# Rotary on VectorE, shared banks read once, and later VectorE halves in the attention mixers of a two-layer decoder

## The chip, the cores and the metric

The kernel runs on one core of a Trainium2 chip. The metric is the device time of one execution in microseconds (us). Unless a number is called a median, it comes from one profiled execution of the kernel; the medians come from runs without a profile.

## What is computed

The input is 256 tokens of width 1024 in fp32. Two layers follow each other; each is a SwiGLU half-step, an attention mixer and a second SwiGLU half-step, every one with an RMSNorm ahead of it and a residual sum behind it. A final RMSNorm ends it. Cut to what matters here:

```python
def partial_rotary(t, pos):                 # first 16 of the 64 columns of every head
    x1, x2 = tf[..., :half], tf[..., half:ROT_DIM]
    out = jnp.concatenate([x1 * cos - x2 * sin, x1 * sin + x2 * cos, tf[..., ROT_DIM:]], axis=-1)

for layer in range(2):
    h = h + 0.5 * swiglu(rmsnorm(h, ffn1_norm[layer]), ...)      # 1024 -> 2816 -> 1024
    hn = rmsnorm(h, mix_norm[layer])
    h = h + (mixer_a(hn, ...) if layer == 0 else mixer_b(hn, ..., shared_k, shared_v))
    h = h + 0.5 * swiglu(rmsnorm(h, ffn2_norm[layer]), ...)
    if layer == 0:
        shared = shared_kv(h, kv_norm, kv_w, pos)
```

With 256 tokens both mixers come down to attention of 16 heads of 64 columns over 256 keys with an additive mask. In mixer A queries, keys and values come from the same normalised stream; in mixer B keys and values come from the stream after layer 0 (with its own norm), queries from the stream of layer 1. Rotary is applied to queries and keys.

## The kernel before, in words

**Split products.** Every fp32 product is made of three fast TensorE matmuls. An operand is split in a rounded part (`hi`, or `wh` for a weight) and a rest (`lo`, `wl`), and `product` (lines 176 to 183) adds hi·hi, hi·lo and lo·hi. ScalarE makes the rounded part by a copy, VectorE the rest by a subtraction that reads source and rounded part: `parts_of` (line 86) for activations, `pieces_of` (line 143) for weights. So a VectorE subtraction always waits for the ScalarE copy of the same tile.

**Stages.** The program runs first half-step, mixer A, half-step, half-step, mixer B, half-step. The half-steps multiply weights as 128x512 matmuls (lines 190 and 193). Only the mixers concern the change; in the profile they lie at about 194 to 342 us and 700 to 838 us.

**A mixer** (line 532) works in four groups `g` of four heads, and in two token tiles `t` of 128 tokens. For a group, `projections` (line 588) yields one product step after another: queries and keys side by side in one 512-wide accumulator per token tile in mixer A (`qk_a`), and the values of both token tiles in the two halves of a third accumulator (`v_a`). In mixer B keys and values share the 512-wide accumulators (`kv_b`) and the queries of both token tiles share one (`q_b`); its last group takes keys, queries and values by themselves (`k_b`, `q_b`, `v_b`). An accumulator is one PSUM bank; there are five of them and three further banks (`trt`) for transposes and scores, each reused in turn.

When a projection is complete, `evacuate` (line 571) reads it: values are split by `parts_of` into `vs`; queries and keys are copied by ScalarE into `turns` (tile `rt`), and when both are there `rotate` (line 456) turns the first 16 columns of every head by four small GpSimd operations (lines 463 to 466). `turn_in` (line 552) transposes `rt` on TensorE (`qt`) and splits the result into `qkh` and `qkl`.

**Attention** (line 468) works on pairs `p` of heads. `scores` multiplies queries and keys (`s`), adds the mask and takes the row minimum on VectorE (line 491), takes the exponential and its sum on ScalarE (line 494), inverts the sums on VectorE (line 496) and scales the rows on GpSimd (line 499). `turn` transposes the result (`pt`) and splits it (`pT`). `values` multiplies it with the values: both heads of a pair have one half each of the accumulator `po`; each half is read by ScalarE and VectorE (lines 522, 523) before the matmuls of the other head, and the sum `oT` is split and appended to `blocks`. `out_t` (line 421) multiplies `blocks` with the output weights.

**What sets the order.** Every engine takes its own instructions strictly in order; semaphores join the engines. The order of the calls is written by `Agenda` (line 252): a clock `now` advances by the cost that each product step yields (0.68 us for a 512-wide step), and a call entered with `after(wait, ...)` is issued when the clock has passed its time. `turn_in` is due 3.6 after its rotary, and when the second token tile is in, `scores`, `turn` and `values` of two pairs are entered with waits from 3.0 to 20.7. `out_t` yields `None` while a block is missing, and the next call is then taken at once. `Pieces` (line 274) splits the weights `LEAD` = 4 pieces ahead of their product step and issues their loads on SP's queue two units ahead of that.

## Time and profile before

| | before |
|---|---|
| median of 3 runs | 1037.94 us (1036.07 to 1038.06) |
| profiled execution, its time | 1037.39 us |
| profiled execution, its span | 1035.3 us |
| instructions in the span | 15836 |
| mean granted TensorE clock | 0.987 of full speed |
| HBM traffic | 174 MB read, 1 MB written, 169 GB/s over the span |

The profile gives for each engine (PE is TensorE's matmul side, PEld its weight loads, DVE VectorE, ACT ScalarE, POOL GpSimd) the busy time and the number of instructions. Its other views, each introduced where it is used, are: a list of waits (which engine's which instruction waited for whom, total, times and longest, in us); a timeline (start and duration in us, engine, source line, operation, tiles written and read, and in brackets the idle time ahead of it and what ended it); groups of instructions of one line and shape (busy time, mean ns of one); and sums over stretches of time (busy time and number of instructions of each engine, the granted clock, the share of the DMA engines, GB/s). Line numbers in profile rows are those of the kernel of that profile. Durations of matmuls include their drain, so two successive starts, not the duration, give the pace.

### The profile page before, as it was taken

How to read it: one execution, taken by the hardware profiler on the slowest of the kernel's cores; microseconds unless marked ns; L12 is line 12 of the kernel's file. 1: busy time of each engine (PE TensorE's matmuls, PEld its weight loads, DVE VectorE, ACT ScalarE, POOL GpSimd, SP SyncE). 2: the span in 40 equal slices, each digit the busy share in tenths (PEclk: the TensorE clock that was granted, in tenths of full speed). 3: DMA queues.
4: the chain of work that ended last, by engine and by line, in shares of the span. 5: the costliest groups of instructions: out<-in, count | busy, mean ns of one | idle time of the engine just before them, and what ended most of it. 6: DMA issues, size and time to landing. Idle time of an engine off the chain costs nothing. (4 is left out here: it accounts for less than half of the span.)

```text
span 1035.3 us, 15836 instructions
## 1 busy us (share of the span) xinstructions
PE 996.0 (96%) x5947; PEld 875.6 (85%) x5947; DVE 714.4 (69%) x1188; ACT 592.7 (57%) x1092; POOL 221.9 (21%) x275
## 2 busy tenths in 40 slices
PE   8999999989879999999999999999898999999997
PEld 5888888878779888888888888888777898888886
DVE  7978866655556787775768877665655677878642
ACT  6765664466456566664546566544665666566531
POOL 3111111252333221110112111111534422111000
PEclk9999999999889999999999999999999999999999
DMA  9775565643223466556655654665433344664521
GB/s 308 257 245 181 183 207 192 200 143 116 82 82 123 163 201 199 170 183 205 195 190 163 193 197 160 213 203 191 146 123 100 104 134 151 204 203 167 205 77 41
DMA packets 158396, 176.05 MB, mean 170 GB/s; under 512 B 3568, under 2 KB 152304, under 8 KB 158320
## 3 DMA queue, kind: packets, MB, share of 16 engines
q1 hardware_dynamic: 157888, 174.50, 50.8%
q8 instruction: 46, 0.75, 0.3%
q10 hardware_dynamic: 432, 0.55, 0.2%
q14 instruction: 30, 0.25, 0.1%
HBM read 173.99 MB, written 1.05 MB: 169 GB/s over the span
## 5 line engine op out<-in xcount | busy, mean ns | idle before, releaser
L190 PE MATMUL f_g<-x_n,wh_f_g 128*128 128x512 f32 x688 | 180.1, 394 | 0.0
L190 PE MATMUL f_u<-x_n,wh_f_u 128*128 128x512 f32 x688 | 177.7, 391 | 2.3 <-DVE j_f_g L321 2.3
L339 POOL TENSOR_TENSOR j_f_u<-j_f_u,r_n 128x256 f32<-128x256 f32 x88 | 77.2, 879 | 381.8 <-DVE j_f_u L321 357.7
L190 PEld LDWEIGHTS f_u<-x_n,wh_f_u 128*128 128x128 f32 x688 | 128.8, 188 | 30.2 <-issue 2.1
L190 PEld LDWEIGHTS f_g<-x_n,wh_f_g 128*128 128x128 f32 x688 | 124.0, 189 | 22.6
L190 PE MATMUL dn_f<-act_f,wh_f 128*128 128x512 f32 x528 | 126.5, 391 | 0.0
L151 DVE TENSOR_TENSOR wl_f_u<-raw_f_u,wh_f_u 128x1024 fp32r<-128x1024 f32 x86 | 119.2, 1387 | 2.8 <-ACT wh_f_u L150 2.7
L151 DVE TENSOR_TENSOR wl_f_g<-raw_f_g,wh_f_g 128x1024 fp32r<-128x1024 f32 x86 | 103.4, 1232 | 19.8 <-PE f_g L193 13.9
L190 PEld LDWEIGHTS dn_f<-act_f,wh_f 128*128 128x128 f32 x528 | 96.8, 188 | 18.6
L151 DVE TENSOR_TENSOR wl_f<-raw_f,wh_f 128x1024 fp32r<-128x1024 f32 x72 | 81.8, 1153 | 35.9 <-ACT wh_f L150 26.7
L193 PE MATMUL f_g<-x_n,wl_f_g 128*128 128x256 f32 x688 | 103.4, 282 | 0.0
L193 PE MATMUL f_u<-x_n,wl_f_u 128*128 128x256 f32 x688 | 103.4, 283 | 0.0
L193 PEld LDWEIGHTS f_g<-x_n,wl_f_g 128*128 128x128 f32 x688 | 96.9, 190 | 6.5
L150 ACT ACTIVATE wh_f<-raw_f 128x1024 fp32r<-128x1024 f32 x72 | 67.3, 978 | 49.5 <-PE dn_f L190 27.2
L150 ACT ACTIVATE wh_f_u<-raw_f_u 128x1024 fp32r<-128x1024 f32 x86 | 86.6, 1046 | 15.0 <-PE f_g L190 10.9
L150 ACT ACTIVATE wh_f_g<-raw_f_g 128x1024 fp32r<-128x1024 f32 x86 | 89.5, 1048 | 9.9 <-issue 6.0
L193 PEld LDWEIGHTS f_u<-x_n,wl_f_u 128*128 128x128 f32 x688 | 91.7, 192 | 0.5 <-DVE wl_f_u L151 0.4
L227 POOL TENSOR_TENSOR ss_n<-ss_n,sq_n 128x256 f32<-128x256 f32 x42 | 41.2, 982 | 210.0 <-ACT sq_n L226 209.0
L88 ACT ACTIVATE act_f<-j_f_g 128x256 fp32r<-128x256 f32 x88 | 36.5, 417 | 71.3 <-DVE j_f_g L340 71.1
L337 ACT ACTIVATE j_f_g<-j_f_g 128x256 f32<-128x256 f32 x88 | 36.8, 418 | 63.1 <-DVE j_f_g L336 62.7
L193 PEld LDWEIGHTS dn_f<-act_f,wl_f 128*128 128x128 f32 x528 | 68.1, 191 | 2.8
L193 PE MATMUL dn_f<-act_f,wl_f 128*128 128x256 f32 x528 | 69.0, 283 | 0.0
(211 smaller groups left out, 1869.3 us busy)
## 6 DMA issues: line engine op xcount, KB each, us to landing
raw_f_g<-in_ffn_w_gate_dram SPq DMA_DIRECT2D x43, 1024.0 KB, 5.2
raw_f_u<-in_ffn_w_up_dram SPq DMA_DIRECT2D x43, 1024.0 KB, 5.2
raw_f<-in_ffn_w_down_dram SPq DMA_DIRECT2D x24, 1024.0 KB, 4.8
raw_f_d<-in_ffn_w_down_dram SPq DMA_DIRECT2D x11, 1024.0 KB, 4.9
raw_f<-in_ffn_w_down_dram SPq DMA_DIRECT2D x12, 768.0 KB, 4.2
raw_qka<-in_a_w_qkv_dram SPq DMA_DIRECT2D x16, 512.0 KB, 4.3
raw_kvb<-in_kv_w_dram SPq DMA_DIRECT2D x12, 512.0 KB, 4.2
raw_va<-in_a_w_qkv_dram SPq DMA_DIRECT2D x4, 1024.0 KB, 5.0
```

Of the source, the lines that this page charges most:

```text
L88: nc.scalar.activation(hi, src, AF.Copy, scale=scale)
L150: nc.scalar.activation(wh, r, AF.Copy)
L151: nc.vector.tensor_sub(wl, r, wh.bitcast(F32))
L190: nc.tensor.matmul(ac, wh, flat(x), start=first and i == 0, stop=False)
L193: nc.tensor.matmul(ac[:, :S], wl, x[:, 0, :], start=False, stop=last and i == len(ws) - 1)
L227: nc.gpsimd.tensor_tensor(self.ss, self.ss, sq, op=ALU.add)
L337: nc.scalar.activation(g, g, AF.Silu)
L339: nc.gpsimd.tensor_tensor(u, u, norm.row, op=ALU.mult)
```

## The change

Five edits, all of them in or for the mixers:

- `rotate` issues its four operations on VectorE, not on GpSimd, and it is entered in the agenda 0.7 after the copy; `turn_in` is due 3.2 after the copy, not 3.6.
- `evacuate` of accumulators that two token tiles share is called when both are complete, so that no matmul goes to a bank between two reads of it; queries and keys that lie side by side are copied in one 512-wide ScalarE operation; in `kv_b` the values are read ahead of the keys.
- `values` issues the matmuls of both heads, then both reads; the VectorE sum, the split of `oT` and its entry in `blocks` become calls of the agenda 0.7, 1.4 and 2.2 later.
- `scores` hands the exponentials (`soften`) and the scaling (`scale`) to the agenda, one head at a time, with a reciprocal for each head.
- The VectorE half of a split is entered 0.7 later (`later=agenda.soon`) in the mixers, and in `Pieces` the subtraction of one piece is issued after the copy of the next one.

`run_next` also sets the clock forward to the time of the call that it takes. The loads on SP's queue stand in the same order in both programs, and away from the mixers every engine's instructions stand in the same order.

```diff
-    def parts_of(hi, lo, src, scale=1.0):
+    def parts_of(hi, lo, src, scale=1.0, later=None):
+        def rest():
+            ...
         nc.scalar.activation(hi, src, AF.Copy, scale=scale)
+        (later or (lambda call: call()))(rest)
...
+        def soon(self, call):
+            self.after(0.7, call)
         def run_next(self):
-            _, call, args = self.calls.pop(0)
+            at, call, args = self.calls.pop(0)
+            self.now = max(self.now, at)
...
-                self.parts.append(pieces_of(f"{name}_{j}", self.raws[u][:, j * k:j * k + k], k, n))
+                nc.scalar.activation(wh, raw, AF.Copy)
+                self.parts.append([(wh[:, r, :], wl[:, r, :]) for r in range(k)])
+                self.rest.append(lambda wl=wl, raw=raw, wh=wh: nc.vector.tensor_sub(wl, raw, wh.bitcast(F32)))
+                while len(self.rest) > (m < end - 1):
+                    self.rest.pop(0)()
...
-        nc.gpsimd.tensor_tensor(ta, v[:, :, :ROT], cs, op=ALU.mult)
-        nc.gpsimd.tensor_tensor(tb[:, :, :HALF], v[:, :, HALF:ROT], sn[:, :, :HALF], op=ALU.mult)
-        nc.gpsimd.tensor_tensor(tb[:, :, HALF:], v[:, :, :HALF], sn[:, :, HALF:], op=ALU.mult)
-        nc.gpsimd.tensor_tensor(v[:, :, :ROT], ta, tb, op=ALU.add)
+        nc.vector.tensor_mul(ta, v[:, :, :ROT], cs)
+        nc.vector.tensor_mul(tb[:, :, :HALF], v[:, :, HALF:ROT], sn[:, :, :HALF])
+        nc.vector.tensor_mul(tb[:, :, HALF:], v[:, :, :HALF], sn[:, :, HALF:])
+        nc.vector.tensor_add(v[:, :, :ROT], ta, tb)
...
+                agenda.after(0.7 + 0.7 * i, soften, sm, nm[:, i], ls[:, i])
+        def soften(sm, nm, ls):
+            ...
+            agenda.after(1.3, scale, sm, ls)
+        def scale(sm, ls):
+            nc.vector.reciprocal(ls, ls)
+            for t, seg in enumerate(segs):
+                nc.gpsimd.tensor_scalar(sm[:, seg], sm[:, seg], ls[:, t:t + 1], None, op0=ALU.mult)
...
+            for own, ac in zip(owns, acs):
                 nc.scalar.activation(s[own], ac[DH:], AF.Copy)
+            agenda.soon(lambda: close(p, s, acs))
+        def close(p, s, acs):
+            for own, ac in zip(owns, acs):
                 nc.vector.tensor_add(s[own], ac[:DH], s[own])
             x = atile([P, 2, S], F32R, name=f"oT_{name}{p}")
-            parts_of(x[:, 0], x[:, 1], s)
+            agenda.soon(lambda: parts_of(x[:, 0], x[:, 1], s, later=agenda.soon))
+            agenda.after(1.5, arrived, x)
...
                 if not missing:
-                    rotate(turns[g, t], t, f"{name}{g}_{t}")
-                    agenda.after(3.6, turn_in, g, t)
+                    agenda.soon(lambda: rotate(turns[g, t], t, f"{name}{g}_{t}"))
+                    agenda.after(3.2, turn_in, g, t)
...
-                            if k0 + 2 * k == KD:
+                            if k0 + 2 * k == KD and wide == 512:
                                 evacuate(g, t, norm.col[t], acs[t], parts, missing[t])
                         i += 2
+                    if wide < 512:
+                        for t in range(NT):
+                            evacuate(g, t, norm.col[t], acs[t], parts, missing[t])
```

The waits of the entries in `turn_in` stay, but for the second `scores` of the first three groups, which is due at 8.0, not 8.5.

More of the change, by code (lines that the diff above doesn't have):

```diff
@@ L84, in flat @@
         return ap.rearrange("p c n -> p (c n)")
-    def parts_of(hi, lo, src, scale=1.0):
+    def parts_of(hi, lo, src, scale=1.0, later=None):
+        def rest():
+            if isinstance(scale, float):
+                nc.vector.tensor_sub(lo, src, hi.bitcast(F32))
+            else:
+                nc.vector.scalar_tensor_tensor(lo, src, scale, hi.bitcast(F32), op0=ALU.mult, op1=ALU.subtract)
         nc.scalar.activation(hi, src, AF.Copy, scale=scale)
-        if isinstance(scale, float):
-            nc.vector.tensor_sub(lo, src, hi.bitcast(F32))
-        else:
-            nc.vector.scalar_tensor_tensor(lo, src, scale, hi.bitcast(F32), op0=ALU.mult, op1=ALU.subtract)
+        (later or (lambda call: call()))(rest)
     def etile(name, dt=F32):
@@ L278, in __init__ @@
         def __init__(self, specs):
-            self.specs, self.raws, self.parts = specs, [], []
+            self.specs, self.raws, self.parts, self.rest = specs, [], [], []
         def load(self, u):
@@ L289, in split @@
         def split(self, i):
-            while len(self.parts) <= min(i, 2 * len(self.specs) - 1):
-                u, j = divmod(len(self.parts), 2)
+            end = 2 * len(self.specs)
+            while len(self.parts) <= min(i, end - 1):
+                m = len(self.parts)
+                u, j = divmod(m, 2)
                 self.load(u + 2)
@@ L294, in split @@
                 k //= 2
-                self.parts.append(pieces_of(f"{name}_{j}", self.raws[u][:, j * k:j * k + k], k, n))
+                raw = self.raws[u][:, j * k:j * k + k]
+                wh, wl = [wp.tile([P, k, n], F32R, tag=tag, name=f"{tag}_{name}_{j}") for tag in ("wh", "wl")]
+                nc.scalar.activation(wh, raw, AF.Copy)
[3 more added lines that the diff above has]
+                    self.rest.pop(0)()
         def __getitem__(self, i):
@@ L462, in rotate, with attention @@
         tb = sp.tile([P, n, ROT], F32, tag="rotb", name=f"rb_{name}", bufs=2)
-        nc.gpsimd.tensor_tensor(ta, v[:, :, :ROT], cs, op=ALU.mult)
-        nc.gpsimd.tensor_tensor(tb[:, :, :HALF], v[:, :, HALF:ROT], sn[:, :, :HALF], op=ALU.mult)
-        nc.gpsimd.tensor_tensor(tb[:, :, HALF:], v[:, :, :HALF], sn[:, :, HALF:], op=ALU.mult)
-        nc.gpsimd.tensor_tensor(v[:, :, :ROT], ta, tb, op=ALU.add)
-    def attention(operands, mask, name, blocks):
+        nc.vector.tensor_mul(ta, v[:, :, :ROT], cs)
+        nc.vector.tensor_mul(tb[:, :, :HALF], v[:, :, HALF:ROT], sn[:, :, :HALF])
+        nc.vector.tensor_mul(tb[:, :, HALF:], v[:, :, :HALF], sn[:, :, HALF:])
+        nc.vector.tensor_add(v[:, :, :ROT], ta, tb)
+    def attention(agenda, operands, mask, name, blocks):
         segs = [slice(t * P, t * P + (t + 1) * P) for t in range(NT)]
@@ L492, in scores @@
                                                    op0=ALU.add, op1=ALU.min, accum_out=nm[:, i, t:t + 1])
-                for t, seg in enumerate(segs):
-                    nc.scalar.activation(sm[:, seg], sm[:, seg], AF.Exp, bias=nm[:, i, t:t + 1], scale=-1.0,
-                                         accum_out=ls[:, i, t:t + 1])
-            nc.vector.reciprocal(flat(ls), flat(ls))
-            for i in range(2):
-                for t, seg in enumerate(segs):
-                    nc.gpsimd.tensor_scalar(sms[p, i][:, seg], sms[p, i][:, seg], ls[:, i, t:t + 1], None, op0=ALU.mult)
+                agenda.after(0.7 + 0.7 * i, soften, sm, nm[:, i], ls[:, i])
+        def soften(sm, nm, ls):
+            for t, seg in enumerate(segs):
+                nc.scalar.activation(sm[:, seg], sm[:, seg], AF.Exp, bias=nm[:, t:t + 1], scale=-1.0,
+                                     accum_out=ls[:, t:t + 1])
+            agenda.after(1.3, scale, sm, ls)
+        def scale(sm, ls):
+            nc.vector.reciprocal(ls, ls)
+            for t, seg in enumerate(segs):
+                nc.gpsimd.tensor_scalar(sm[:, seg], sm[:, seg], ls[:, t:t + 1], None, op0=ALU.mult)
         def turn(p, i):
@@ L504, in turn @@
                 nc.tensor.transpose(tr[:, n * P:(n + 1) * P], sms[p, i][:, n * P:(n + 1) * P], ident)
-            pT = pp.tile([P, 2, 3 * P], F32R, tag="pT", name=f"pT_{name}{p}_{i}")
-            parts_of(pT[:, 0], pT[:, 1], tr)
-            pTs[p, i] = pT
+            pT = pTs[p, i] = pp.tile([P, 2, 3 * P], F32R, tag="pT", name=f"pT_{name}{p}_{i}")
+            parts_of(pT[:, 0], pT[:, 1], tr, later=agenda.soon)
         def values(p):
@@ L513, in values @@
             vs = operands(g)[1]
-            for i, own in enumerate(owns):
+            acs = [po[:, i * S:(i + 1) * S] for i in range(2)]
+            for i, ac in enumerate(acs):
                 pT = pTs[p, i]
                 v0, v1 = [flat(v[:, 2 * b + i]) for v in vs]
-                ac = po[:, i * S:(i + 1) * S]
                 for n in range(2):
@@ L521, in values, with arrived @@
                     nc.tensor.matmul(ac[:, P:], v1, pT[:, n, S:], start=False, stop=n == 1)
+            for own, ac in zip(owns, acs):
                 nc.scalar.activation(s[own], ac[DH:], AF.Copy)
+            agenda.soon(lambda: close(p, s, acs))
+        def close(p, s, acs):
+            for own, ac in zip(owns, acs):
                 nc.vector.tensor_add(s[own], ac[:DH], s[own])
             x = atile([P, 2, S], F32R, name=f"oT_{name}{p}")
-            parts_of(x[:, 0], x[:, 1], s)
+            agenda.soon(lambda: parts_of(x[:, 0], x[:, 1], s, later=agenda.soon))
+            agenda.after(1.5, arrived, x)
+        def arrived(x):
             blocks.append(x)
@@ L549, in mixer @@
         agenda = Agenda()
-        scores, turn, values = attention(lambda g: (qks[g], vss[g]), mask, name, blocks)
+        scores, turn, values = attention(agenda, lambda g: (qks[g], vss[g]), mask, name, blocks)
         def turn_in(g, t):
@@ L559, in turn_in @@
                 nc.tensor.transpose(tr[:, k * P:(k + 1) * P], s[:, k * P:(k + 1) * P], ident)
-            parts_of(*[x[:, :, t, :] for x in qks[g]], tr.rearrange("p (k n) -> p k n", n=P))
+            parts_of(*[x[:, :, t, :] for x in qks[g]], tr.rearrange("p (k n) -> p k n", n=P), later=agenda.soon)
             if t == NT - 1:
                 p = 2 * g
-                for wait, call, args in ((3.0, scores, (p,)), (8.5, scores, (p + 1,)), (11.0, turn, (p, 0)),
+                for wait, call, args in ((3.0, scores, (p,)), (8.0, scores, (p + 1,)), (11.0, turn, (p, 0)),
                                          (12.3, turn, (p, 1)), (15.0, values, (p,)), (17.0, turn, (p + 1, 0)),
@@ L571, in evacuate @@
         def evacuate(g, t, r, ac, parts, missing):
-            for m, (kind, _, _) in enumerate(parts):
-                src = ac[:, m * n:(m + 1) * n]
-                if kind == "v":
-                    v = atile([P, HG, 2, DH], F32R, name=f"vs_{name}{g}_{t}")
-                    vss.setdefault(g, []).append(v)
-                    parts_of(v[:, :, 0], v[:, :, 1], src.rearrange("p (j d) -> p j d", d=DH), r)
-                    continue
-                if (g, t) not in turns:
-                    turns[g, t] = atile([P, 2 * HG, DH], name=f"rt_{name}{g}_{t}")
-                slots = slice(0, HG) if kind == "q" else slice(HG, 2 * HG)
-                nc.scalar.activation(flat(turns[g, t][:, slots]), src, AF.Copy, scale=r)
-                missing.discard(kind)
+            if (g, t) not in turns:
+                turns[g, t] = atile([P, 2 * HG, DH], name=f"rt_{name}{g}_{t}")
+            kinds = [kind for kind, _, _ in parts]
+            if kinds[-1] == "v":
+                v = atile([P, HG, 2, DH], F32R, name=f"vs_{name}{g}_{t}")
+                vss.setdefault(g, []).append(v)
+                src = ac[:, (len(kinds) - 1) * n:]
+                parts_of(v[:, :, 0], v[:, :, 1], src.rearrange("p (j d) -> p j d", d=DH), r, later=agenda.soon)
+                kinds.pop()
+            if kinds:
+                slots = turns[g, t][:, 0 if kinds[0] == "q" else HG:HG if kinds[-1] == "q" else 2 * HG]
+                nc.scalar.activation(flat(slots), ac[:, :len(kinds) * n], AF.Copy, scale=r)
+                missing.difference_update(kinds)
                 if not missing:
-                    rotate(turns[g, t], t, f"{name}{g}_{t}")
-                    agenda.after(3.6, turn_in, g, t)
+                    agenda.soon(lambda: rotate(turns[g, t], t, f"{name}{g}_{t}"))
+                    agenda.after(3.2, turn_in, g, t)
         def projections():
@@ L606, in projections @@
                                 yield 0.68 if wide == 512 else 0.36
-                            if norm.col is None and (t == NT - 1 or k0 + 2 * k == KD):
+                            if norm.col is None and t == NT - 1:
                                 norm.finish()
-                            if k0 + 2 * k == KD:
+                            if k0 + 2 * k == KD and wide == 512:
                                 evacuate(g, t, norm.col[t], acs[t], parts, missing[t])
                         i += 2
+                    if wide < 512:
+                        for t in range(NT):
+                            evacuate(g, t, norm.col[t], acs[t], parts, missing[t])
         agenda.run(projections())
```

## The prediction

> **What bounds the kernel now.** I read the page's busy times first, then TensorE's waits, then the stretches around the longest of them.

> ```profile
> span 1035.3 us, 15836 instructions
> PE 996.0 (96%) x5947; PEld 875.6 (85%) x5947; DVE 714.4 (69%) x1188; ACT 592.7 (57%) x1092; POOL 221.9 (21%) x275
> ```

> TensorE is busy for 96% of the span and sets the end; its idle time is 39 us. The list of its waits says where (engine, instruction, releaser, then total, times and longest):

> ```profile
> PE qt_a L559 <- POOL rt_a L466: 10.2, 4, 3.4
> PE qt_b L559 <- POOL rt_b L466: 7.7, 3, 3.0
> PE q_b L179 <- ACT rt_b L582: 2.8, 4, 1.6
> PE po_b L519 <- DVE o_b L523: 2.2, 2, 1.9
> PE v_a L179 <- DVE vs_a L92: 2.1, 3, 0.8
> PE po_a L519 <- DVE o_a L523: 1.9, 4, 1.1
> ```

> All six rows lie in the two mixers. The first two, 17.9 us, are the transpose of queries and keys waiting for the rotary on GpSimd. The other four, 9.0 us, are matmuls that wait to write one half of a bank while ScalarE or VectorE still reads the other half. Together 26.9 us.

> One of the long ones in the timeline, GpSimd first, then TensorE:

> ```profile
> 225.47 3.94 POOL L499 TENSOR_SCALAR sm_a<-sm_a,ls_a 128x128 f32<-128x128 f32 x4 [1.11 <-DVE ls_a L496]
> 229.38 0.45 POOL L463 TENSOR_TENSOR ra_a<-rt_a,rot 128x128 f32<-128x128 f32 x1
> 229.79 1.30 POOL L464 TENSOR_TENSOR rb_a<-rt_a,rot 128x64 f32<-128x64 f32 x1
> 231.05 0.32 POOL L465 TENSOR_TENSOR rb_a<-rt_a,rot 128x64 f32<-128x64 f32 x1
> 231.44 0.45 POOL L466 TENSOR_TENSOR rt_a<-ra_a,rb_a 128x128 f32<-128x128 f32 x1
> ...
> 231.95 1.11 PE L559 MATMUL qt_a<-ident,rt_a 128*128 128x128 f32 x4 [3.21 <-POOL rt_a L466]
> ```

> The rotary stands on GpSimd's queue behind 3.94 us of softmax scaling, itself takes 2.5 us, and TensorE stands still for 3.21 us.

> A stall costs more than its length. Sums over stretches (length, PE, PEld, DVE, ACT and POOL busy, granted clock):

> ```profile
> 230.82:231.95 1.13, 0.00 (x0) 0.00 (x1) 0.09 (x1) 0.00 (x0) 1.05 (x4) 0.50 0.00 0
> 231.95:237.65 5.70, 5.70 (x27) 5.70 (x28) 1.11 (x2) 0.98 (x2) 1.37 (x4) 0.50 0.51 184
> 262.78:268.37 5.59, 5.59 (x26) 5.59 (x27) 1.11 (x2) 0.98 (x2) 1.37 (x4) 0.50 0.50 188
> 293.67:299.09 5.42, 5.42 (x26) 5.42 (x27) 1.11 (x2) 0.98 (x2) 1.37 (x4) 0.50 0.59 193
> 814.50:817.91 3.41, 3.41 (x18) 3.41 (x17) 2.17 (x11) 2.43 (x9) 1.37 (x2) 0.50 0.02 5
> ...
> 755.00:782.00 27.00, 23.52 (x170) 20.29 (x169) 16.49 (x38) 17.64 (x41) 11.57 (x16) 1.00 0.33 116
> ```

> Within each of the three long stalls of mixer A the granted clock falls to half, and it stays there for 5.4 to 5.7 us of matmul work behind the stall. In mixer B a stall of 3.0 us costs no clock (last row, which holds one), but the `po_b` wait of 1.9 us is followed by 3.41 us at half. Work at half clock takes twice its time, so half of 5.70 + 5.59 + 5.42 + 3.41 = 20.1 us is lost: 10.1 us.

> **The change part by part.**

> *Rotary off GpSimd.* This removes the cause of the 17.9 us. VectorE has no such small rotary row, so I bound it by its nearest rows:

> ```profile
> L496 DVE RECIPROCAL ls_a<-ls_a 128x4 f32<-128x4 f32 x8 | 1.4, 177 | 4.9 <-ACT sm_a L494 4.9
> L243 DVE TENSOR_SCALAR diag_n<-ident,c_n 128x128 f32<-128x128 f32 x8 | 1.9, 284 | 3.1 <-POOL c_n L236 3.1
> L336 DVE TENSOR_TENSOR j_f_g<-j_f_g,r_n 128x256 f32<-128x256 f32 x88 | 39.5, 452 | 1.2
> ```

> Four elements take 177 ns, 128 take 284 ns and 256 take up to 452 ns; so four operations take between 0.7 us (4 x 177) and 1.8 us (4 x 452). I take 1.0 us (2 x 284 and 2 x about 220 for the 64-element ones, between the first two rows). A group has two rotaries, so VectorE gets 2.0 us more per group. The row of one group period of mixer A, from one qt stall to near the next:

> ```profile
> 238.70:269.50 30.80, 26.55 (x160) 22.73 (x158) 17.14 (x39) 17.27 (x41) 11.82 (x16) 0.89 0.29 103
> 370.00:690.00 320.00, 319.56 (x1839) 282.00 (x1839) 238.14 (x365) 182.90 (x310) 46.68 (x51) 1.00 0.58 191
> ```

> Without its long stall (3.4 us), its `v_a` wait (0.7) and its half clock (half of 5.59, 2.8) this period is 23.9 us; VectorE then has 17.1 + 2.0 = 19.1 us in it, 80%, and ScalarE's 17.3 us are 72%. In the half-steps (second row) VectorE is busy for 238 of 320 us, 74%, and TensorE never waits. So VectorE is covered, but with a margin of less than 5 us per group, and it takes its work in order.

> Is the rotary in time? The rows for the pace (successive starts) of matmuls, of six transposes and of half a `po`; for the way from the mask to the last exponential of a pair (its first and last row, 14 between); and for copies and a subtraction:

> ```profile
> 239.50 0.40 PE L179 MATMUL qk_a<-wh_qka,x_n 128*128 128x512 f32 x1
> 239.73 0.39 PE L181 MATMUL qk_a<-wl_qka,x_n 128*128 128x512 f32 x1
> ...
> 242.10 0.28 PE L181 MATMUL v_a<-wl_va,x_n 128*128 128x256 f32 x1
> 242.22 0.28 PE L183 MATMUL v_a<-wh_va,x_n 128*128 128x256 f32 x1
> ...
> 742.35 0.82 PE L504 MATMUL pt_b<-ident,sm_b 128*128 128x128 f32 x6
> 742.92 0.47 PE L179 MATMUL kv_b<-wh_kvb,x_kx 128*128 128x512 f32 x1
> ...
> 237.85 0.48 PE L519 MATMUL po_a<-pT_a,vs_a 128*128 128x256 f32 x2
> 238.17 0.34 PE L521 MATMUL po_a<-pT_a,vs_a 128*128 128x128 f32 x2
> 238.34 0.62 PE L504 MATMUL pt_a<-ident,sm_a 128*128 128x128 f32 x4
> ...
> 217.16 0.28 DVE L491 CUSTOM_DVE_ANT_0 sm_a<-s_a,masks 128x128 f32<-128x128 f32 x1
> ...
> 219.16 0.19 ACT L494 ACTIVATION_READ_ACCUMULATOR sm_a<-sm_a,nm_a 128x1 f32 x1
> ...
> L582 ACT ACTIVATE rt_b<-q_b,c_n 128x256 f32<-128x256 f32 x8 | 3.8, 470 | 3.8 <-POOL c_n L236 2.4 <-PE q_b L183 1.4
> L88 ACT ACTIVATE qkh_a<-qt_a 128x512 fp32r<-128x512 f32 x8 | 4.8, 598 | 14.5 <-PE qt_a L559 14.5
> L151 DVE TENSOR_TENSOR wl_qka<-raw_qka,wh_qka 128x1024 fp32r<-128x1024 f32 x16 | 19.6, 1231 | 8.7 <-ACT wh_qka L150 8.3
> ```

> In mixer A count from the end of the first token tile's `qk`. TensorE has 12 matmuls of the other tile, six transposes and six value matmuls before `qt`: 12 x 0.23 + 0.57 + 6 x 0.12 = 4.0 us. The scores of a pair end nine matmuls (2.1 us) before that point; mask and exponentials take 219.35 - 217.16 = 2.2 us, and a weight subtraction may hold them up by half its length, 0.6 us: ScalarE is free at 0.7 us, the 512-wide copy takes 0.6 and the rotary 1.0, ready at 2.3 us. Slack 1.7 us: one weight subtraction of 1.23 us in front of it would still be hidden, two would not. In mixer B the order on VectorE puts one weight subtraction between the last two operations of the second token tile's rotary: ready at about 0.1 + 0.9 (two copies) + 1.8 (seven operations) + 1.2 = 4.0 us, TensorE there after 9 x 0.23 + 0.98 (`po`, twice 238.34 - 237.85) + 6 x 0.23 + 0.3 = 4.7 us. Slack 0.7 us. In its last group VectorE has the mask rows of a pair in between as well, and I get 0.3 to 0.5 us too late.

> *Banks read when complete.* Takes the 9.0 us away: no matmul goes to those banks between two reads. In its place the reads come later, so banks come free later. The copies in front of `qt` are two short ones (0.9 us, above). I see no bank reused within 2 us of its read among the five accumulators; among the three transpose banks one pair in mixer B (scores behind `pt_b`) is within 0.3 us.

> *VectorE's half a step later.* Splits reach TensorE later by one piece of four (a piece feeds 12 matmuls, 12 x 0.23 = 2.7 us, so three pieces, 8 us, remain as lead). Source tiles come free a piece later too, so SP issues the next load later; the queue's order stays, a load lands in 4.3 us (row below) and is issued two units, some 11 us, ahead.

> ```profile
> raw_qka<-in_a_w_qkv_dram SPq DMA_DIRECT2D x16, 512.0 KB, 4.3
> ```

> What the edit buys is that VectorE's head-of-line waits for ScalarE (8.7 us in the `wl_qka` row) shrink, which is what makes room for the rotary. I cost it at nothing; its cover is that lead, and if it were gone the price would be up to one 1.23 us subtraction per piece.

> *The softmax by heads.* 16 more reciprocals at 177 ns, 0.35 us per group, inside the 4.8 us left of VectorE's group. The first head's scaling starts about 1 us earlier.

> *The half clock.* It goes with the stalls: 10.1 us.

> *What stays.* I expect some four places with 0.3 to 0.5 us (three in mixer B, one at the end of mixer A), 1.5 us, and as much again for places where the in-order queue is later than my count: 3 us, with no extra half clock. From below it is 0; from above, with half a microsecond at each of the 16 turn-ins, 8 us, and with a half-clock stretch of 3.41 us (1.7 us lost) behind two of them 11.4 us.

> Sum: the profiled execution took 1037.39 us; 1037.39 - 26.9 - 10.1 + 3.0 = 1003.4 us. Its time lies 0.55 us under the median of 1037.94 us, which changes nothing here. I predict **1003.5 us**.

> [...]

> **The rivals.**

> *VectorE becomes late.* The stall moves from GpSimd's queue to VectorE's: at 80% and in order, the rotary stands behind a subtraction that waits for ScalarE. For it: the slack of 0.7 us in mixer B and the 8.7 us that VectorE waits at `wl_qka`. Against it: the half-steps at 74% without any wait. Price: 0.5 us at 16 turn-ins and the clock as above, 11.4 in place of 3 us: **1012 us**.

> *The bank waits stay.* If what makes TensorE wait is not the read between two halves but the reader's lateness, the 9.0 us only move to the next user of the bank, and the half clock behind `po_b` (1.7 us) with them: 1003.5 + 10.7 = **1014 us**. Against it: five accumulators, and after the change the next user of a bank comes a projection later. This is also the case in which that edit does not do what it says.

> *Slower.* In the timeline above one 64-element rotary operation took 1.30 us where its twin took 0.32 us, while VectorE ran a subtraction: the two disturb each other. Should the strided rotary cost VectorE as much, 4 x 1.3 = 5.2 us each, a group gets 10.4 us more and VectorE needs 17.1 + 10.4 = 27.5 us; if it still waits for others in 4.8 of the 13.7 us that it is idle now, that makes 32.3 us against a period of 30.8 us before. Eight groups then lose 1.5 us each: 1037.4 + 12 = **1049 us**. It decides from about 1.1 us per operation (17.1 + 8.9 + 4.8 = 30.8). Against it: no VectorE row of this size is above 0.45 us, and GpSimd's own two-input work leaves the mixers with the rotary.

> **How the numbers follow.** Forecast 72%; VectorE late 15%; bank waits stay 7%; slower 4%; about no change, with the gains lost in new places, 2%. The range for 8 in 10 goes from 999.5 (nothing stays: 1000.4, less 0.9 for the spread of the runs) to 1013 us, over the first rival and most of the second. 0.2%, about 2 us, is what a measurement of this kernel can tell from no change: faster 94%, same 2%, slower 4%.

> **What would show it.** Right: no wait of `qt` above 0.7 us, now on VectorE, and in all under 4 us; no wait of `q_b`, `v_a` and `po` on a read; granted clock 1.0 in the mixers; TensorE's busy time down by about 10 us; VectorE with 64 + 16 instructions more, GpSimd with 64 fewer; rotary operations of 0.2 to 0.3 us. Wrong: rotary operations of over 0.5 us, `qt` waiting for VectorE by a microsecond and more, half clock behind such a wait, or new waits of TensorE on `wl` or on transpose banks.

## The result and the profile after

The changed kernel takes **996.38 us** (median of 4 runs, 996.36 to 996.49), the kernel before on the same chip 1038.0 us (4 runs, 1036.07 to 1039.29): a ratio of 0.960 (95% interval 0.958 to 0.962). That is 41.6 us less, where the prediction had 34.4, and 3 us below the low end of its range. The profiled execution took 996.37 us.

The busy times of the profile after:

```profile
span 994.6 us, 15837 instructions
...
PE 981.1 (99%) x5947; PEld 866.7 (87%) x5947; DVE 728.4 (73%) x1268; ACT 590.8 (59%) x1084; POOL 177.1 (18%) x211
```

TensorE has 13.5 us of idle time left, where it had 39. VectorE has 80 instructions more, GpSimd 64 fewer. TensorE's waits (engine, instruction, releaser, then total, times and longest):

```profile
PE pt_b L526 <- DVE nm_b L508: 1.4, 1, 1.4
...
PE po_a L540 <- DVE o_a L549: 0.3, 1, 0.3
PE po_b L540 <- DVE o_b L549: 0.3, 1, 0.3
```

The six rows of the prediction are gone, but for 0.3 us at the last `po` of each mixer; of the rows that are left only `pt_b`'s 1.4 us is new. The rotary now, first as groups (busy, mean ns of one), then in the timeline of mixer A (the first token tile of its second group) and of mixer B (the second token tile of its third group):

```profile
L482 DVE TENSOR_TENSOR rt_a<-ra_a,rb_a 128x128 f32<-128x128 f32 x8 | 2.4, 299 | 0.3
L479 DVE TENSOR_TENSOR ra_a<-rt_a,rot 128x128 f32<-128x128 f32 x8 | 2.3, 287 | 2.7 <-ACT rt_a L612 2.7
...
L481 DVE TENSOR_TENSOR rb_a<-rt_a,rot 128x64 f32<-128x64 f32 x8 | 1.8, 230 | 0.0
L480 DVE TENSOR_TENSOR rb_a<-rt_a,rot 128x64 f32<-128x64 f32 x8 | 1.8, 225 | 0.0
```

```profile
225.86 0.34 DVE L482 TENSOR_TENSOR rt_a<-ra_a,rb_a 128x128 f32<-128x128 f32 x1
...
227.86 0.60 PE L588 MATMUL qt_a<-ident,rt_a 128*128 128x128 f32 x4
...
745.32 0.21 DVE L481 TENSOR_TENSOR rb_b<-rt_b,rot 128x64 f32<-128x64 f32 x1
745.46 1.21 DVE L309 TENSOR_TENSOR wl_bo<-raw_bo,wh_bo 128x1024 fp32r<-128x1024 f32 x1
746.59 0.28 DVE L482 TENSOR_TENSOR rt_b<-ra_b,rb_b 128x128 f32<-128x128 f32 x1
...
747.03 1.04 PE L588 MATMUL qt_b<-ident,rt_b 128*128 128x128 f32 x8
```

The rotary in mixer A is ready at 226.20, 1.7 us ahead of its transposes; at the first token tiles of its four groups it is 1.6, 1.7, 0.8 and 0.8 us ahead. The eight transposes of mixer B are those of both token tiles, and the four of the second one start at 747.46. Its rotary is ready at 746.87, 0.6 us ahead, behind one weight subtraction. One group period of mixer A, and all of mixer A with its output projection (length, PE, PEld, DVE, ACT and POOL busy, granted clock):

```profile
231.74:254.70 22.96, 22.96 (x158) 20.02 (x157) 17.79 (x48) 16.67 (x38) 6.07 (x8) 1.00 0.40 136
...
193.00:312.00 119.00, 118.17 (x838) 106.00 (x837) 88.93 (x217) 82.11 (x177) 31.69 (x38) 1.00 0.44 142
```

The clock is 1.00 in both mixers.

### The profile page after: what moved, and what is told of

The parts are those of the page before. It is cut to its first block, busy times and chain, and to the rows that moved or that the text cites. A ratio compares the mean times of both kernels' runs of the same rounds, so it can differ in the third digit from the quotient of the medians.

```text
span 994.6 us, 15837 instructions
## 1 busy us (share of the span) xinstructions
PE 981.1 (99%) x5947; PEld 866.7 (87%) x5947; DVE 728.4 (73%) x1268; ACT 590.8 (59%) x1084; POOL 177.1 (18%) x211
## 3 DMA queue, kind: packets, MB, share of 16 engines
HBM read 173.99 MB, written 1.05 MB: 176 GB/s over the span
## 5 line engine op out<-in xcount | busy, mean ns | idle before, releaser
L153 ACT ACTIVATE wh_f_g<-raw_f_g 128x1024 fp32r<-128x1024 f32 x86 | 89.5, 1048 | 10.4 <-issue 6.0
L153 ACT ACTIVATE wh_f_u<-raw_f_u 128x1024 fp32r<-128x1024 f32 x86 | 86.7, 1047 | 15.1 <-PE f_g L193 10.8
## 6 DMA issues: line engine op xcount, KB each, us to landing
raw_qka<-in_a_w_qkv_dram SPq DMA_DIRECT2D x16, 512.0 KB, 4.2
raw_kvb<-in_kv_w_dram SPq DMA_DIRECT2D x12, 512.0 KB, 4.2
```

Of the source, the lines that this page charges most:

```text
L153: nc.scalar.activation(wh, r, AF.Copy)
```

## The experiments

The questions: does the part that the prediction missed belong to an edit that it costed at nothing (called theory B in the expectations), or did it read too little out of the rows it had (theory A)? First the changed kernel with one edit undone at a time, then the kernel before with one edit alone, then a test of the clock, then tries for a faster version. The kernel before ran beside all of them, with medians of 1038.1 to 1039.6 us; differences below are of medians unless they are called profiled. The kernels did not all run on one chip, so a difference of a few tenths of a microsecond to the changed kernel's 996.38 us says little.

A measure that all of them share: between the start of one matmul and the start of the next lies the pace of its shape (0.227 us for 512 columns, 0.12 for 256), or more. I took each tile and shape's pace (the lower quartile of successive starts in the trace of before) off every step in the two mixers, and sorted what is left by what the trace says of the step: a listed idle time over 0.1 us, half clock, or neither. All in us, from the profiled execution of each kernel:

| kernel | its time | idle listed (over 0.1) | the same steps in full | half clock | other steps | sum of the last three |
|---|---|---|---|---|---|---|
| before | 1037.39 | 27.7 | 32.2 | 9.8 | 31.5 | 73.4 |
| before, rotary on VectorE (d1) | 1011.38 | 10.3 | 14.2 | 0 | 33.3 | 47.5 |
| before, banks read whole (d2) | 1018.74 | 17.1 | 19.7 | 5.9 | 29.1 | 54.7 |
| after, rotary on GpSimd (u1) | 1009.69 | 11.4 | 13.2 | 3.0 | 29.4 | 45.6 |
| after, banks read by halves (u2) | 1010.71 | 11.2 | 14.8 | 0 | 32.1 | 46.9 |
| after, values alone by halves (u5) | 1009.31 | 9.1 | 12.2 | 1.8 | 29.9 | 43.9 |
| after, projections alone (u6) | 1002.90 | 5.9 | 7.5 | 0 | 31.8 | 39.2 |
| after, softmax by pairs (u4) | 998.80 | 4.7 | 6.3 | 0 | 28.6 | 34.9 |
| after | 996.37 | 2.9 | 4.2 | 0 | 28.7 | 32.9 |

The difference of a row's sum to that of the last row follows the time within 0.7 us everywhere (before: 40.5 of 41.0 us) but in u5, where it is 11.0 of 12.9 us. Most of the rest there lies outside the program's span, which is 3.4 us shorter than the time of that execution, against 1.8 us after the change; the spans themselves differ by 11.3 us. So the mixers hold nearly all of the gain. The listed idle time alone holds 24.8 of the 41 us.

### One edit undone: the rotary (u1)

```diff
-        nc.vector.tensor_mul(ta, v[:, :, :ROT], cs)
+        nc.gpsimd.tensor_tensor(ta, v[:, :, :ROT], cs, op=ALU.mult)
...
```

> The changed kernel (996.4 us) with the rotary alone put back on GpSimd. Theory A (the 7 us by which the prediction fell short are waits that the wait list understates, some 0.16 us each, and short ones that it leaves out): the qt waits return behind GpSimd, 2 to 3 us at 7 of the 16 turn-ins, with half clock behind the three of mixer A; 1013 to 1024 us, and the time lost exceeds listed waits plus half clock by about 0.16 us for each wait that returns. Theory B (the 7 us come from an edit that the prediction costed at nothing, the later halves or the softmax by heads): the time lost equals listed waits plus half clock, at most 27 us, and nothing is left over. Theory C (with the scaling issued by heads and earlier, GpSimd would have been in time): under 1003 us.

1009.46 us (1008.15 to 1011.13), 13.1 more than the changed kernel: less than theory A expected, and more than theory C's 1003 us. Its waits:

```profile
PE qt_a L588 <- POOL rt_a L482: 7.3, 3, 3.0
...
PE qt_b L588 <- POOL rt_b L482: 1.8, 4, 0.8
```

Mixer A's waits come back at three of its turn-ins, up to 3.0 us long; mixer B's do not (1.8 us where the kernel before had 7.7). So something else in the change had taken most of those, and d2 below shows what. Of the 13.3 us between the profiled executions the table places 8.5 in listed idle time, 0.5 more in the same steps, 3.0 in half clock and 0.7 in other steps. There are three listed steps more than after the change, so the 0.5 us are 0.16 for each.

### One edit undone: the banks (u2), and its two halves (u5, u6)

```diff
-                            if k0 + 2 * k == KD and wide == 512:
+                            if k0 + 2 * k == KD:
                                 evacuate(g, t, norm.col[t], acs[t], parts, missing[t])
                         i += 2
-                    if wide < 512:
-                        for t in range(NT):
-                            evacuate(g, t, norm.col[t], acs[t], parts, missing[t])
...
                 for n in range(2):
                     nc.tensor.matmul(ac[:, P:], v1, pT[:, n, S:], start=False, stop=n == 1)
-            for own, ac in zip(owns, acs):
-                nc.scalar.activation(s[own], ac[DH:], AF.Copy)
+                nc.scalar.activation(s[owns[i]], ac[DH:], AF.Copy)
+                nc.vector.tensor_add(s[owns[i]], ac[:DH], s[owns[i]])
...
         def close(p, s, acs):
-            for own, ac in zip(owns, acs):
-                nc.vector.tensor_add(s[own], ac[:DH], s[own])
```

u2 has both edits, u6 only the first (the projections), u5 only the second (`values` and `close`). With the second the VectorE sum is no longer entered later either.

> The changed kernel with the bank edit alone undone: each half of a shared bank is read as soon as it is complete. Theory A: the 16 waits return, 9.0 us listed and some 2.5 us more that is not listed, and perhaps a half-clock stretch (1.7 us): 1006 to 1010 us. Theory B: at most what is listed, 9 us, so 1003 to 1005.5 us. Rival that the bank waits were due to late readers: the readers are in time now, under 1001 us.

> Half of the bank edit undone: only the two heads' values are read each as soon as it is complete; the projections are still read whole. Theory A (a wait at a bank costs what is listed and some 0.25 us more, and switches too short for the list add to it): the po waits return with some 7 us listed, and the time rises by 9.5 to 11.5 us, to 1006 to 1008 us. Theory B (the list is complete, the rest of the 15 us comes from elsewhere): up by 7 us, 1003.5 us, no more.

> The other half of the bank edit undone: only the 256-wide projections are read token tile by token tile, the values whole. Theory A: the q_b and v_b waits return with some 3 us listed, the time rises by 4 to 6 us, to 1000.5 to 1002.5 us, and with the half above it adds up to the 15.1 us of both. Theory B: up by 3 us, 999.5 us.

Measured: u2 1011.49 us (+15.1), u5 1008.07 (+11.7), u6 1003.20 (+6.8). All three lie above what the list of waits explains; u2 and u6 also lie above what theory A expected, u5 at the top of it. Together u5 and u6 cost 18.5 us, more than u2, so the costs of the two halves overlap. Between the profiled executions u2 costs 14.3 us: the table places 8.3 in listed idle time, 2.3 more in the same steps and 3.4 in other steps. The longest waits of u2:

```profile
PE po_a L540 <- DVE o_a L544: 3.7, 6, 1.1
PE po_b L540 <- DVE o_b L544: 3.3, 5, 1.4
PE q_b L182 <- ACT rt_b L610: 2.6, 3, 1.1
```

One of them in its timeline:

```profile
241.03 0.40 PE L182 MATMUL qk_a<-wh_qka,x_n 128*128 128x512 f32 x1
...
241.26 0.39 PE L184 MATMUL qk_a<-wl_qka,x_n 128*128 128x512 f32 x1
...
241.73 0.38 ACT L543 ACTIVATE o_a<-po_a 64x256 f32<-64x256 f32 x1
...
242.14 0.42 DVE L544 TENSOR_TENSOR o_a<-po_a,o_a 64x256 f32<-64x256 f32 x1 [0.24 <-ACT o_a L543]
...
242.61 0.50 PE L540 MATMUL po_a<-pT_a,vs_a 128*128 128x256 f32 x2 [0.96 <-DVE o_a L544]
```

The list gives this wait 0.96 us. But the matmul at 241.26 has a record of 0.39 us, and its successor could have started 0.23 us behind it, at 241.49; it started at 242.61. The stop costs 1.12 us: the list counts idle time only from the end of the record, and the last 0.16 us of the record are the part that in a running stream overlaps the next matmul. A stop shorter than that isn't listed at all, and TensorE counts as busy in it. In u6 mixer A has no listed wait of `v_a`, and its other steps still take 2.0 us more than after the change; 1.8 of them lie at the steps that enter `v_a` from another tile. Those are stops at a bank that the list doesn't show. In u2 the steps that enter a shared bank from another tile hold 1.7 of the short steps' 3.4 us; what lengthens the rest stays open.

### One edit undone: the later halves (u3), the softmax by heads (u4)

```diff
-        (later or (lambda call: call()))(rest)
+        rest()
...
-                while len(self.rest) > (m < end - 1):
+                while self.rest:
```

> The changed kernel with VectorE's half of every split issued at once behind ScalarE's, as before. Theory A (the later halves only make room): 0 to 3 us, 996.5 to 999.5 us, all of it in listed waits, most at qt, and VectorE idle behind ScalarE's copies as before. Theory B (the later halves are what the prediction missed): 3 to 7 us and more, 999.5 to 1004 us, with few listed waits.

996.92 us (996.85 to 997.01), 0.5 us more (by the profiled spans, 994.8 and 994.6 us, 0.2), and no wait of `qt` over 0.2 us. This rules out theory B for this edit.

In u4 `scores` issues the softmax of both heads at once:

```diff
-                agenda.after(0.7 + 0.7 * i, soften, sm, nm[:, i], ls[:, i])
+                for t, seg in enumerate(segs):
+                    nc.scalar.activation(sm[:, seg], sm[:, seg], AF.Exp, ...)
+            nc.vector.reciprocal(flat(ls), flat(ls))
+            for i in range(2):
+                for t, seg in enumerate(segs):
+                    nc.gpsimd.tensor_scalar(sms[p, i][:, seg], sms[p, i][:, seg], ls[:, i, t:t + 1], None, op0=ALU.mult)
```

> The changed kernel with the softmax of a pair issued in one go, as before (exponentials of both heads, one reciprocal, four scalings). Theory A: 0 to 2 us, 996.5 to 998.5 us, a wait of pt for the scaling at the most. Theory B (the softmax by heads is what the prediction missed): 3 us and more, over 999.5 us.

998.66 us, 2.3 us more, most of it in two waits of mixer A's last stretch:

```profile
PE pt_a L532 <- POOL sm_a L516: 1.8, 2, 0.9
```

The transposes wait there for GpSimd's scaling, which begins later when it waits for both heads. The 2.3 us are 0.3 more than theory A allowed and short of theory B's 3.

### One edit alone: the rotary (d1), the banks (d2)

d1 is the kernel before with the four rotary lines on VectorE:

```diff
-        nc.gpsimd.tensor_tensor(ta, v[:, :, :ROT], cs, op=ALU.mult)
+        nc.vector.tensor_mul(ta, v[:, :, :ROT], cs)
...
```

> The kernel before with the rotary alone moved to VectorE. Theory A: the qt waits (17.9 us listed, 19.1 with 0.17 us more for each of the 7) and the half clock of mixer A (8.4 us) go, bank waits and their half clock (1.7 us) stay: 1010 to 1014 us if VectorE is in time without the later halves. Rival (without them VectorE's queue is late): qt waits of 1 us and more on VectorE, over 1014 us. If the unlisted part is nothing: 1011.5 us or more.

1012.18 us (1011.08 to 1014.01): 27.1 us less than before (ratio 0.975, 0.972 to 0.979) and within theory A's 1010 to 1014 us, and without the later halves no wait of `qt` appears. The bank waits all stay:

```profile
PE q_b L179 <- ACT rt_b L582: 2.8, 4, 1.6
PE po_b L519 <- DVE o_b L523: 2.5, 3, 1.9
...
PE po_a L519 <- DVE o_a L523: 2.0, 4, 1.1
PE v_a L179 <- DVE vs_a L92: 1.6, 3, 0.6
```

From here to the changed kernel are 15.0 us in the profiled executions, for the bank edit, the softmax by heads and the later halves together. The table splits them: 7.4 listed, 2.6 more in the listed steps, 4.6 in steps without a listed wait.

d2 is the kernel before with the reads of shared banks moved behind the second half's matmuls:

```diff
-                            if k0 + 2 * k == KD:
+                            if k0 + 2 * k == KD and wide == 512:
                                 evacuate(g, t, norm.col[t], acs[t], parts, missing[t])
                         i += 2
+                    if wide < 512:
+                        for t in range(NT):
+                            evacuate(g, t, norm.col[t], acs[t], parts, missing[t])
...
+            for i, own in enumerate(owns):
+                ac = po[:, i * S:(i + 1) * S]
                 nc.scalar.activation(s[own], ac[DH:], AF.Copy)
+            for i, own in enumerate(owns):
+                ac = po[:, i * S:(i + 1) * S]
                 nc.vector.tensor_add(s[own], ac[:DH], s[own])
```

> The kernel before with the bank edit alone: halves that share a bank are read when both are complete. Theory A: its 16 waits go, 9.0 us listed and some 2.5 us not listed, with 1.7 us of half clock, unless the time is lost again at qt, where GpSimd is the late one: the qt waits grow by what the bank waits in front of them gave. 1025 to 1031 us. Theory B: 1027 to 1031 us. Rival that the waits only move on to the next user of the bank: 1036 to 1040 us.

1018.76 us (1018.34 to 1019.80): 20.5 us less (ratio 0.981, 0.978 to 0.986), 6 us more than any theory had. Its waits:

```profile
PE qt_a L563 <- POOL rt_a L466: 10.5, 3, 3.8
PE qt_b L563 <- POOL rt_b L466: 2.8, 5, 1.0
```

Reading `q_b` whole takes 4.9 of mixer B's 7.7 us of `qt_b` waits away without touching the rotary. One of the long stalls of before, then GpSimd and TensorE in d2 at the same place:

```profile
750.93 0.66 PE L559 MATMUL qt_b<-ident,rt_b 128*128 128x128 f32 x4 [3.01 <-POOL rt_b L466]
```

```profile
736.52 3.51 POOL L499 TENSOR_SCALAR sm_b<-sm_b,ls_b 128x128 f32<-128x128 f32 x4 [1.78 <-PE pt_b L504]
740.00 0.46 POOL L463 TENSOR_TENSOR ra_b<-rt_b,rot 128x128 f32<-128x128 f32 x1
...
742.08 0.46 POOL L466 TENSOR_TENSOR rt_b<-ra_b,rb_b 128x128 f32<-128x128 f32 x1
```

```profile
743.18 0.60 PE L563 MATMUL qt_b<-ident,rt_b 128*128 128x128 f32 x4
```

The rotary still stands behind 3.5 us of scaling, but TensorE asks for it later: the plan counts 3.6 us from the copy, and the first token tile's copy now comes after the second tile's matmuls. So GpSimd is done at 742.54 and TensorE asks at 743.18. The gains of the two edits alone, 27.1 + 20.5 = 47.6 us, exceed what all edits together gain (41.6 us, or 42.9 against the 1039.28 us of the kernel before beside d1 and d2), because such waits go with either.

### The clock (d3)

```diff
             tr = trt(f"qt_{name}{g}_{t}")
+            if name == "a" and g and t == 0:
+                for _ in range(11):
+                    nc.tensor.matmul(tr, fill[:, :P], fill, start=True, stop=True)
```

> The kernel before with 11 matmuls of constants (some 2.4 us) put into the qt bank ahead of the transposes of the first token tile in groups 1 to 3 of mixer A, where TensorE stands still for 3.2 to 3.4 us and the clock falls; their result is overwritten. The stall stays as long, only TensorE is busy in most of it. If the half clock is a consequence of the idle time: the three stretches at 0.50 vanish and the kernel gains 7.5 to 8.5 us, 1029 to 1031 us. If the clock falls for another reason: no gain, 1036 to 1039 us.

1033.60 us (10 runs, 1031.77 to 1036.57), 5.7 us less than before (ratio 0.995, 0.993 to 0.997): a gain, but short of the 7.5 to 8.5 us expected. In mixer A the clock stays at 1.00 (mean over 193 to 312 us), as expected of a clock that follows the idle time. But in the profiled execution it now falls in mixer B, where the trace of before had none at the same stalls:

```profile
740.21:743.62 3.41, 0.43 (x5) 0.43 (x5) 1.69 (x2) 0.95 (x2) 3.33 (x6) 1.00 0.07 13
743.62:747.03 3.41, 3.41 (x13) 2.83 (x11) 0.69 (x1) 0.60 (x1) 0.95 (x3) 0.50 0.84 294
767.51:770.93 3.42, 1.39 (x12) 1.19 (x10) 2.00 (x2) 2.23 (x3) 3.34 (x6) 1.00 0.00 0
770.93:777.75 6.82, 5.86 (x28) 5.86 (x29) 1.71 (x3) 0.98 (x2) 2.33 (x5) 0.50 0.48 154
```

At half clock TensorE works 3.41 and 5.86 us; I estimate that half of it, 4.6, is lost (in the trace of before, 9.8 us of 20.1 us of such work, where 256-wide matmuls start 0.21 us apart instead of 0.12). Of the 9.8 us of half clock before, 8.0 lay in mixer A and 1.8 in mixer B. So 8.0 - (4.6 - 1.8) = 5.2 us were to be gained, and the profiled executions differ by 1037.39 - 1032.22 = 5.2.

What makes the clock fall, then? The length of a stop doesn't settle it. In d2 a stop of 3.20 us costs no clock, where before the same stop of 3.21 us did; in d1 a `po_b` wait of 1.92 us costs none, where before the wait of 1.92 us at the same place did. The rows of d2, then of before, then of d1, each time the wait in the timeline and then sums over stretches of 3.41 us:

```profile
231.80 0.66 PE L563 MATMUL qt_a<-ident,rt_a 128*128 128x128 f32 x4 [3.20 <-POOL rt_a L466]
...
226.56:229.98 3.42, 2.04 (x15) 1.68 (x13) 2.69 (x4) 2.62 (x6) 3.42 (x5) 1.00 0.16 53
229.98:233.39 3.41, 1.59 (x14) 1.59 (x15) 1.05 (x2) 0.60 (x1) 3.13 (x7) 1.00 0.38 111
```

```profile
812.79 0.50 PE L519 MATMUL po_b<-pT_b,vs_b 128*128 128x256 f32 x2 [1.92 <-DVE o_b L523]
...
811.09:814.50 3.41, 1.71 (x14) 1.51 (x15) 1.82 (x3) 2.50 (x7) 2.24 (x3) 1.00 0.91 299
```

```profile
788.36 0.50 PE L519 MATMUL po_b<-pT_b,vs_b 128*128 128x256 f32 x2 [1.92 <-DVE o_b L523]
...
783.75:787.16 3.41, 2.69 (x22) 2.28 (x21) 2.45 (x10) 1.85 (x8) 0.00 (x0) 1.00 0.17 40
787.16:790.58 3.42, 2.22 (x19) 2.02 (x20) 2.28 (x5) 2.04 (x6) 2.75 (x4) 1.00 0.79 270
```

### Tries for a faster version (b1, b2, b3)

The longest wait left is `pt_b`'s 1.4 us, whose bank is held by scores that VectorE reads late. b1 and b2 move the last pair's scores in the last group's list:

```diff
-                                         (3.0, scores, (p,)), (5.0, scores, (p + 1,)), (9.5, turn, (p, 0)),
+                                         (3.0, scores, (p,)), (4.0, scores, (p + 1,)), (9.5, turn, (p, 0)),
```

(b1; b2 has 7.0.)

> A try at the longest wait that is left (1.4 us, a transpose of mixer B's last stretch whose bank is held by scores that VectorE reads late, behind a weight subtraction): the last pair's scores issued a step and a half earlier (4.0 in place of 5.0), so that VectorE reads them ahead of that subtraction. If the wait is the reader's place in VectorE's queue it goes: 994.5 to 995.5 us. If it moves to another bank user: 996 to 997 us.

> The other way round: the last pair's scores issued later (7.0 in place of 5.0), behind more transposes of the group before. If that transpose gets its bank ahead of the scores the wait goes, 994.5 to 996 us; if the softmax of the last pair becomes late for its own transposes, they wait instead: 996 to 999 us.

b1 took 996.67 us, b2 998.97. In b1 the `pt_b` wait is gone, and a `po_b` waits 1.0 us in its place; in b2 `s_b` waits 1.2 us and `pt_a` 1.3 for the scaling. b3 is b1 with VectorE's half of `pT` issued at once.

```diff
-            parts_of(pT[:, 0], pT[:, 1], tr, later=agenda.soon)
+            parts_of(pT[:, 0], pT[:, 1], tr)
```

> The try with the last pair's scores earlier, and VectorE's half of the transposed softmax issued at once instead of half a microsecond of plan later. In that try the second half of a po stood 0.97 us because this half lay behind a weight subtraction on VectorE. If that place in the queue is the cause, the wait falls to 0.2 us or less and nothing takes its place: 995 to 995.9 us, under the 996.4 us of the changed kernel. If VectorE now waits at its head for ScalarE's copy and is late elsewhere: 996.4 us or more.

996.56 us, and the same wait of 0.97 us. VectorE, then TensorE in b3:

```profile
779.57 1.23 DVE L154 TENSOR_TENSOR wl_f_g<-raw_f_g,wh_f_g 128x1024 fp32r<-128x1024 f32 x1 [0.78 <-ACT wh_f_g L153]
780.71 0.55 DVE L90 TENSOR_TENSOR pT_b<-pt_b,pT_b 128x384 fp32r<-128x384 f32 x1
```

```profile
781.32 0.39 PE L540 MATMUL po_b<-pT_b,vs_b 128*128 128x256 f32 x1 [0.97 <-DVE pT_b L90]
```

The subtraction of the next half-step's weights still stands ahead of `pT`'s half: taking the delay out did not bring that half ahead of it, so the delay was not what put it behind. None of the three beats the changed kernel.

## Why the prediction was right in direction and wrong in size

**Rotary off GpSimd: right.** The prediction took 17.9 us of waits and the half clock behind them. d1 measures it alone: 26.0 us between the profiled executions (18.0 of waits in full, 9.8 of half clock, less 1.8 by which other steps grew). The duration of a rotary was estimated at 1.0 us; the four rows sum to 287 + 225 + 230 + 299 = 1041 ns. The slack in mixer A was put at 1.7 us and is 1.6 to 1.7 us in two groups, 0.8 in the other two; in mixer B it was put at 0.7 us and is 0.6 in the third group, with the one weight subtraction between the last two operations that the prediction named. The group period was to be 23.9 us with VectorE at 80%; it is 22.96 us and 17.79 / 22.96 = 77%.

**Banks read when complete: the step that failed.** "Takes the 9.0 us away" took the totals of the four bank rows as the whole price. Undone, the edit costs 15.1 us, 14.3 between the profiled executions (u2). The mechanism was right: the rows are gone but for the 0.3 us at each mixer's last `po`, and the rival by which the waits only move to the next user did not happen.

The term was too small for two reasons, both in how the list was read. A stop costs more than is listed, in the trace of before 0.16 to 0.17 us and, behind score matmuls, 0.27: in u2 2.3 of the 14.3 us. The prediction's own rows showed it, with records of 0.39 us at a pace of 0.23. And 3.4 us lie in steps that the list doesn't show at all: half of them, and nearly all in mixer A of u6, at the entry of a shared bank.

From d1 to after, with the other edits, the sum had 9.0 us of waits less the 3.0 that stay, and 15.0 were measured; the softmax by heads, below, is the other part of that.

The profile models the ends of matmuls, so the ends behind 0.39 - 0.23 = 0.16 us are no measurement of their own; the starts are. The unlisted time also explains TensorE's busy time, which fell by 14.9 us where the prediction allowed only 10, for the clock.

**The range.** Its low end took "nothing stays", 1000.4 us, for a bound, but listed waits are a lower bound of what stops cost, so no sum of them bounds the gain.

**The half clock: right sum, wrong certainty.** 10.1 us were forecast and 9.8 went. The forecast rested on one execution, though: the grid lies differently in the profiles (a step begins at 230.82 us in before, 229.98 in d2 and 743.62 in d3, that is 2.1, 1.3 and 2.9 us behind a multiple of 3.413), and the kernel before took 1034.11 to 1044.04 us in 13 runs beside d1, with mean granted clocks of 0.992 and 0.979 in these two, while the changed kernel, with no stop over 1.4 us, stays within 0.13 us. The prediction gave the drop at 814.50 us to the wait of 1.9 us ahead of it, and its 1.7 us did go. But d1 shows the same wait without a drop and d2 a stop of 3.20 us without one, so the prediction's reading by lengths does not decide it.

**The later halves: cost right, purpose wrong.** They cost nothing, as forecast, and bring 0.5 us at most. But they are not "what makes room for the rotary": without them `qt` does not wait either (u3, d1).

**The softmax by heads: undervalued.** Costed as 0.35 us per group on VectorE, and in the sum at nothing; it is worth 2.3 us, 1.8 of them waits for the scaling in mixer A's last stretch (u4).

**What stays: right, for other places.** 3 us were forecast; the waits over 0.1 us in the mixers sum to 2.9, of which 1.0 was there before (0.4 of the norm, 0.3 at each last `po`). The `qt` waits of 0.3 to 0.5 us in mixer B's last group are 0.12 and 0.13. The 1.4 us are on a transpose bank: a `pt_b` waits there until the scores are read. The prediction counted a pair there as within 0.3 us, in the other order.

## What to carry to other kernels

Read TensorE's stops from start to start against the pace of the shape, not from the idle column: short stops look like busy time, and what the idle column leaves out can weigh as much as what it lists (in u6, 3.3 us beside 3.0). When two edits remove the same wait, each alone looks bigger than its share; undo and do each before giving a gain to one of them. Where runs scatter with the granted clock, look at the stops: the kernel before spread over 1034.11 to 1044.04 us at mean clocks of 0.992 to 0.979, and with its stops closed four runs lie within 0.13 us.

## What the runs showed of the hardware

The clock fell behind a stop of 1.43 us in u5 and not behind one of 3.20 us in d2. In u5 that single wait was followed by 3.41 us at half clock (in the rows over a stretch the granted clock is the third number from the end):

```profile
291.68 0.50 PE L540 MATMUL po_a<-pT_a,vs_a 128*128 128x256 f32 x2 [1.43 <-DVE o_a L544]
...
289.39:292.81 3.42, 1.99 (x20) 1.00 0.86 280
292.81:296.22 3.41, 3.41 (x20) 0.50 0.08 27
```

The rotary's two-input operations on 128 partitions, with strided operands, took 217 to 230 ns (64 elements a partition) and 283 to 299 ns (128) on VectorE, as means after the change. On GpSimd the single ones before took 0.31 to 1.4 us and 0.45 to 1.5 us.
